# A new order for the opening of a decoder layer: conditioning rows behind the tokens, a fifth weight buffer, and all tokens turned between the first two channel tiles

## The chip, the cores and the metric

The kernel runs on one core of a Trainium2 chip. A core has a matrix engine (TensorE, PE in the profile), a vector engine (VectorE, DVE), a scalar engine (ScalarE, ACT), GpSimd (POOL) and SyncE (SP), which here only issues transfers. Each engine works through its own instructions in order. Sixteen DMA engines move data between the chip's memory (HBM) and the on-chip memory (SBUF). Matmul results go to PSUM.

The metric is the device time of one execution in microseconds (us): the median of several runs.

## What is computed

One layer of a hybrid decoder on 256 tokens with 2048 channels, all in float32, and a final norm. The parts that matter here:

```python
c_act = jax.nn.silu(c)
mod = jnp.dot(c_act, w_ada[l]) + b_ada[l]
shift1, scale1, gate1, shift2, scale2, gate2 = jnp.split(mod, 6, axis=-1)
h = _modulate(_rms_norm(x, norm1_g[l]), shift1, scale1)
proj = jnp.einsum("bsd,de->bse", h, w_in[l])
lru_x, lru_gate, q, k, v, g_a, g_b = jnp.split(proj, split_idx, axis=-1)
...
merged = jax.nn.sigmoid(g_a) * y_a + jax.nn.sigmoid(g_b) * y_b
x = x + gate1[:, None, :] * jnp.einsum("bsd,de->bse", merged, w_out[l])
h2 = _modulate(_rms_norm(x, norm2_g[l]), shift2, scale2)
ff = jnp.square(jax.nn.relu(jnp.einsum("bsd,df->bsf", h2, w_ff1[l])))
x = x + gate2[:, None, :] * jnp.einsum("bsf,fd->bsd", ff, w_ff2[l])
...
return _rms_norm(x, final_g)
```

`_rms_norm` divides each token by the root of its mean square and multiplies by a gain; `_modulate` is `h * (1 + scale) + shift`. Before the first weight of `w_in` can be used, the kernel therefore needs the statistics of all tokens, and for each tile of 128 channels its shift and its scale, each a product of the conditioning vector with 128 rows of `w_ada`.

## The kernel before

**Layout.** Channels lie on the 128 partitions in 16 tiles (`KT = 16`), tokens along the free dimension (256). The tokens come as rows, so they are turned on TensorE: four quarters of 512 channels, each quarter two channel tiles.

**Precision.** A float32 product is made of three faster ones: weight and activation are each split into a rounded part and a rest (`wh`, `wl`; `h[j][:, 0]`, `h[j][:, 1]`), and three of the four products are added. For a weight tile ACT makes the rounded part (L161) and DVE the rest (L163), in halves of 1024 columns; for a channel tile L146 and L147. One kind of unit, the native one (L206), uses the raw weights and needs no split.

**Conditioning.** A row of `w_ada` for one tile is 128 x 2048 values, 1 MB, and is multiplied with the line of the activated conditioning vector (`scr`) and summed on DVE (L287, `ada_unit`). There are 96 such rows; rows 0 and 1 are the shift and scale of channel tile 0, rows 2 and 3 those of tile 1, and so on.

**Buffers.** Conditioning rows and weight tiles share one tag (`raw`), with `RAW_BUFS = 4` buffers of 1 MB. A transfer into a buffer is issued on SP's queue once the buffer's last reader is done: L287 for a conditioning row, L163 for a weight tile. The tokens lie first in the buffers of `wh` and `wl`. Pairs of channel tiles (normalised tokens, their splits, results) share the pool `kp` with 49 buffers.

**The opening**, in program order: the vector table `vc` and the identity `idt` come on ACT's queue, the tokens in four transfers on SP's, and behind them conditioning rows 0 and 1, the first weights, and row 2. The conditioning line is made by four groups of transposes (`line_quarter`, L225, L226), between which DVE and ACT sum the squares of the tokens (L229, L233). `rstd_cols` makes the factors `rs1`. `turn_in(q)` scales a quarter (DVE for the first 128 tokens, L254, ACT for the others, L255), turns it by 8 transposes (L261) and evicts it by two copies (L263). `norm1_tile(j)` makes the factor of tile j on DVE (L301), applies it on ACT (L303) and splits the tile.

**The order.** `pin` (`keep_in_program_order`) keeps the marked instructions of an engine in the order of the program. The rest, the matmuls among it, is put in order by a scheduler when the kernel is built, by priority (program order) and by when its model expects an instruction's inputs; it also hands out the pool's buffers as they come free. The pinned order of the opening is the last part of the code below, L307 to L323.

**Passes and units.** The input projection begins before all channel tiles exist: `PASSES = [(0, 2, 56), (2, 6, 56), (6, 10, 40)]` goes over channel tiles 0 and 1 for 56 output tiles, then 2 to 5, then 6 to 9; a pass evicts or adds its part into `res` (L372, L374, L376). One transfer of 1 MB is a unit: 7 in pass 1, 14 in pass 2, 10 in pass 3. In pass 1 a unit is 8 output tiles by 2 channel tiles by 3 matmuls, 48 in all, with 4 PSUM banks for the output tiles. Between units conditioning rows are reduced (`ADA_FIRST`), those of rows 4 to 11 pinned. Then come the rest of the projection, attention and recurrence, the two branch projections, the output projection, and four groups of feed-forward units; the remaining conditioning rows are spread among them.

Of the kernel before, what the change touches and what calls it, by code (L numbers as in the profile page):

```python
# [58 lines left out]
def hybrid_layer(ctx: ExitStack, tc: tile.TileContext, x, xt, wada, w_p, w_r, w_f, vec, lruw, relb,  # L59
# [22 lines left out]
    def tmp(shape=(P, 2, T), dt=F32):  # L82
        return tp.tile(list(shape), dt, tag="t2", name=nm("t"))
# [59 lines left out]
    def split(src, pin=lambda i: i):  # L143

        hl = pair(F32R)
        pin(se.activation(hl[:, 0], src, AF.Copy))  # L146
        pin(ve.tensor_tensor(out=hl[:, 1], in0=src, in1=hl[:, 0].bitcast(F32), op=ALU.subtract))  # L147
        return hl


    def w_dma(src, n, pin=lambda i: i):
        raw = wp.tile([P, 2048], F32, tag="raw", name=nm("rw"), bufs=RAW_BUFS)
        pin(nc.sync.dma_start(out=raw[:, :n], in_=src))
        return raw, n

    def w_split(raw, n, pin=lambda i: i, o0=0):
        parts = []
        for o in range(o0, o0 + n, WCH):
            c = min(WCH, o0 + n - o)
            wh = wp.tile([P, WCH], F32R, tag="wh", name=nm("wh"), bufs=WH_BUFS)  # L160
            pin(se.activation(wh[:, :c], raw[:, o:o + c], AF.Copy))  # L161
            wl = wp.tile([P, WCH], F32R, tag="wl", name=nm("wl"), bufs=WH_BUFS)
            pin(ve.tensor_tensor(out=wl[:, :c], in0=raw[:, o:o + c], in1=wh[:, :c].bitcast(F32), op=ALU.subtract))  # L163
            parts.append((wh, wl))
# [55 lines left out]
    def line_quarter(q):  # L220
# [4 lines left out]
            te.transpose(pc[:, i * P:(i + 1) * P], sc[:, k:k + 1].broadcast_to((P, P)), idt)  # L225
        pin(se.activation(scr[:, q * 512:(q + 1) * 512], pc, AF.Copy))  # L226

    def square_dve(b, q):
        pin(ve.tensor_tensor_reduce(out=tmp([P, 512]), in0=xtok[b, q], in1=xtok[b, q], scale=1.0, scalar=0.0,  # L229
                                    op0=ALU.mult, op1=ALU.add, accum_out=ssq[:, b, q:q + 1]))  # L230

    def square_act(b, q):
# [16 lines left out]
    rs1 = rstd_cols(ss1, pin)  # L249
    xs = []  # L250

    def turn_in(q):

        pin(ve.tensor_scalar(out=xtok[0, q], in0=xtok[0, q], scalar1=rs1[:, 0:1], scalar2=None, op0=ALU.mult))  # L254
        pin(se.activation(xtok[1, q], xtok[1, q], AF.Copy, scale=rs1[:, 1:2]))  # L255
        for j in (2 * q, 2 * q + 1):
            px = bank([P, 512])
            for i in range(2):
                for b in range(2):
                    e = (2 * (j % 2) + i) * P  # L260
                    te.transpose(px[:, i * T + b * P:i * T + (b + 1) * P], xtok[b, q][:, e:e + P], idt)  # L261
            xs.append(pair())
            pin(se.activation(xs[j].rearrange("p a b -> p (a b)"), px, AF.Copy))  # L263
# [4 lines left out]
    same = lambda i: i  # L268

    def ada_dma(pin=same):  # L270
        raw = wp.tile([P, KT * P], F32, tag="raw", name=nm("ra"), bufs=RAW_BUFS)
        pin(nc.sync.dma_start(out=raw, in_=wada[ada_next[0] + len(ada_raw)]))
        ada_raw.append(raw)

    ada_raw = []

    def ada_unit(pin=same):
# [7 lines left out]
        if 2 * PASSES[0][1] <= n < 2 * PASSES[0][1] + 8:  # L285
            pin = tc.keep_in_program_order
        pin(ve.tensor_tensor_reduce(out=raw, in0=raw, in1=scr, scale=1.0, scalar=vc[:, V_BADA + c:V_BADA + c + 1],  # L287
                                    op0=ALU.mult, op1=ALU.add, accum_out=mod[:, c:c + 1]))
        return n

# [3 lines left out]
    def ada_norm1():  # L294
        n = ada_unit()
        if n % 2 == 1:
            norm1_tile(n // 2)

    def norm1_tile(j, pin=same):
        xj = xs[j // 2][:, j % 2]  # L300
        pin(ve.scalar_tensor_tensor(out=a1[:, j:j + 1], in0=mod[:, KT + j:KT + j + 1], scalar=1.0,  # L301
                                    in1=vc[:, V_G1 + j:V_G1 + j + 1], op0=ALU.add, op1=ALU.mult))
        pin(se.activation(xj, xj, AF.Identity, scale=a1[:, j:j + 1], bias=mod[:, j:j + 1]))  # L303
        h[j] = split(xj, pin)
# [633 lines left out]
```

## Time and profile before

| | us |
|---|---|
| median of 3 runs | 1588.19 |
| lowest, highest | 1587.64, 1589.57 |
| the profiled execution | 1585.86 |
| its span, first to last instruction | 1584.1 |
| mean granted clock of TensorE | 0.992 of full |

How to read the rows in the prediction: a timeline row gives the start, the duration, the engine, the line of the code, the operation, what it writes and reads, how many instructions are merged, and in brackets how long the engine was idle before it and what released it. A row of a view by stretches gives the stretch, its length, and busy time and number of instructions of each engine; then the granted clock of TensorE (1.00 is full), the busy share of the DMA engines, and GB/s. A row "A <- B: x, n, y" of the list of waits says that A waited for B for x us in n times, the longest y.

### The profile page before, as it was taken

What the parts mean: (1) busy time and instruction counts of PE and PEld (TensorE: products, weight loads), DVE (VectorE), ACT (ScalarE), POOL (GpSimd) and SP (SyncE); (2) the same over time, 40 slices, a digit from 0 to 9 for tenths busy, and PEclk for the clock granted to TensorE, in tenths of its full rate; (3) what the DMA queues carried; (4) which work ended last, traced back from release to release, by engine and by line L of the source; (5) the groups of instructions that cost most, each with busy time, mean ns of one, the idle gap of its engine ahead of it and who ended that gap; (6) DMA issues with size and microseconds to landing.
All of it is one profiled execution on the core that took longest, in us unless ns stands there. A gap on an engine that the chain in (4) does not pass through costs nothing.

```text
span 1584.1 us, 24932 instructions
## 1 busy us (share of the span) xinstructions
PE 1543.9 (97%) x9812; PEld 1383.8 (87%) x9812; DVE 1216.9 (77%) x1941; ACT 890.9 (56%) x1510; POOL 0.2 (0%) x4
## 2 busy tenths in 40 slices
PE   4999999999999999999999999999999999999997
PEld 4999998899988888888889988888888888888886
DVE  5898998898989879788898877965665556655664
ACT  5733447687796564445455863356434663356553
POOL 0000000000000000000000000000000000000000
PEclk7999999999999999999999999999999999999999
DMA  8998976557767768777886666875555555555552
GB/s 324 343 341 321 337 277 210 204 181 242 282 247 291 266 240 301 283 292 288 322 313 239 229 247 249 331 256 190 194 192 189 190 186 186 186 186 188 188 188 75
DMA packets 61126, 387.90 MB, mean 245 GB/s; under 512 B 6512, under 2 KB 10960, under 8 KB 18640
## 3 DMA queue, kind: packets, MB, share of 16 engines
q1 hardware_dynamic: 55728, 380.66, 66.1%
q10 hardware_dynamic: 5280, 5.64, 1.2%
q8 instruction: 77, 1.26, 0.3%
q14 instruction: 41, 0.34, 0.1%
HBM read 384.13 MB, written 2.15 MB: 244 GB/s over the span
## 4 chain that ended last, share of the span: by engine, by line
PE 86%; DVE 5%; DMA 4%; issue 3%; ACT 2%; ACTq 0%; DVEq 0%
PE pg L191 41%; PE pg L190 20%; PE pg L179 5%; PE pg L177 5%; PE pg L178 5%; DMA ra<-in_wada_dram 3%; DVE wl L163 2%; PE pg L206 2%; PE pg L193 1%; PE pg L727 1%; PE pg L728 1%; PE pg L726 1%; DVE ra L287 1%; PE pa L532 1%; PE pa L539 1%
## 5 line engine op out<-in xcount | busy, mean ns | idle before, releaser
L191 PE MATMUL pg<-k,wh 128*128 128x512 f32 x3120 | 1076.0, 394 | 0.3 <-DVE k L147 0.3
L163 DVE TENSOR_TENSOR wl<-rw,wh 128x1024 fp32r<-128x1024 f32 (+2 forms) x534 | 628.3, 1179 | 266.1 <-ACT wh L161 259.8
L161 ACT ACTIVATE wh<-rw 128x1024 fp32r<-128x1024 f32 (+2 forms) x534 | 545.0, 1022 | 509.0 <-PE pg L191 353.3
L190 PE MATMUL pg<-k,wl 128*128 128x256 f32 x2925 | 818.9, 280 | 0.6 <-DVE wl L163 0.6
L191 PEld LDWEIGHTS pg<-k,wh 128*128 128x128 f32 x3120 | 572.6, 188 | 118.9 <-PE pg L191 0.6
L190 PEld LDWEIGHTS pg<-k,wl 128*128 128x128 f32 x2925 | 550.3, 188 | 10.4 <-DVE wl L163 0.9
L177 PE MATMUL pg<-k,wh 128*128 128x256 f32 x832 | 237.6, 287 | 7.4 <-ACT k L146 5.7
L179 PE MATMUL pg<-k,wl 128*128 128x256 f32 x832 | 233.6, 284 | 3.6 <-DVE wl L163 3.6
L287 DVE CUSTOM_DVE_ANT_0 ra<-ra,scr,vc 128x2048 f32<-128x2048 f32 x96 | 225.1, 2346 | 14.4 <-DMA ra<-in_wada_dram 14.3
L178 PE MATMUL pg<-k,wh 128*128 128x256 f32 x832 | 234.2, 282 | 0.0
L177 PEld LDWEIGHTS pg<-k,wh 128*128 128x128 f32 x832 | 157.5, 190 | 10.0 <-ACT k L146 6.5
L179 PEld LDWEIGHTS pg<-k,wl 128*128 128x128 f32 x832 | 156.5, 189 | 6.2 <-DVE wl L163 4.9
L178 PEld LDWEIGHTS pg<-k,wh 128*128 128x128 f32 x832 | 157.5, 189 | 0.7 <-issue 0.3
L754 DVE SCALAR_TENSOR_TENSOR k<-pg,mod,k 128x256 f32<-128x256 f32 x128 | 61.9, 484 | 31.7 <-PE pg L191 29.5
L743 ACT ACTIVATE t<-t 128x256 f32<-128x256 f32 x55 | 23.0, 419 | 68.0 <-DVE t L198 67.8
L193 PE MATMUL pg<-k,wl 128*128 128x256 f32 x195 | 54.7, 281 | 2.0 <-DVE wl L163 2.0
L198 DVE TENSOR_TENSOR t<-pg,t 128x256 f32<-128x256 f32 x131 | 54.8, 418 | 0.0
L197 ACT ACTIVATE t<-pg 128x256 f32<-128x256 f32 x131 | 47.8, 365 | 1.7 <-PE pg L191 1.7
L193 PEld LDWEIGHTS pg<-k,wl 128*128 128x128 f32 x195 | 36.6, 188 | 10.8 <-DVE wl L163 2.8
L727 PE MATMUL pg<-z,wh 128*128 128x256 f32 x144 | 41.0, 285 | 0.0
L726 PE MATMUL pg<-z,wh 128*128 128x258 f32 x144 | 40.7, 282 | 0.0
L728 PE MATMUL pg<-z,wl 128*128 128x258 f32 x144 | 40.6, 282 | 0.0
(161 smaller groups left out, 963.1 us busy)
## 6 DMA issues: line engine op xcount, KB each, us to landing
rw<-in_w_f_dram SPq DMA_DIRECT2D x204, 1024.0 KB, 4.8
ra<-in_wada_dram SPq DMA_DIRECT2D x96, 1024.0 KB, 6.2
rw<-in_w_p_dram SPq DMA_DIRECT2D x31, 1024.0 KB, 6.4
rw<-in_w_r_dram SPq DMA_DIRECT2D x20, 768.0 KB, 4.5
rw<-in_w_r_dram SPq DMA_DIRECT2D x16, 640.0 KB, 3.9
bt<-ud ACTq DMA_DIRECT2D x8, 512.0 KB, 4.0
lw<-in_lruw_dram SPq DMA_DIRECT2D x4, 512.0 KB, 5.9
k<-in_x_dram SPq DMA_DIRECT2D x8, 256.0 KB, 6.0
```

Source lines behind the costliest of these rows:

```text
L161: pin(se.activation(wh[:, :c], raw[:, o:o + c], AF.Copy))
L163: pin(ve.tensor_tensor(out=wl[:, :c], in0=raw[:, o:o + c], in1=wh[:, :c].bitcast(F32), op=ALU.subtract))
L177: te.matmul(ps, lhsT=wh[:, w], rhs=hl[:, 0], start=k == 0, stop=False)
L178: te.matmul(ps, lhsT=wh[:, w], rhs=hl[:, 1], start=False, stop=False)
L179: te.matmul(ps, lhsT=wl[:, w], rhs=hl[:, 0], start=False, stop=k == n - 1)
L190: te.matmul(ps[:, 0], lhsT=wl[:, w], rhs=hl[:, 0], start=False, stop=False)
L191: te.matmul(ps, lhsT=wh[:, w], rhs=hl, start=k == 0, stop=k == n - 1)
L193: te.matmul(ps[:, 0], lhsT=wl[:, w], rhs=hl[:, 0], start=False, stop=False)
L287: pin(ve.tensor_tensor_reduce(out=raw, in0=raw, in1=scr, scale=1.0, scalar=vc[:, V_BADA + c:V_BADA + c + 1], op0=ALU.mult, op1=ALU.add, ac ...
L726: te.matmul(ps, lhsT=wh[:, e], rhs=z[k][:, 0:258], start=k == 0, stop=False)
L727: te.matmul(ps[:, 0:256], lhsT=wh[:, e], rhs=z[k][:, 258:514], start=False, stop=False)
L754: ve.scalar_tensor_tensor(out=x1[f], in0=ps[:, i], scalar=mod[:, 5 * KT + f:5 * KT + f + 1], in1=x1[f], op0=ALU.mult, op1=ALU.add)
```

## The change

It has four parts.

1. `RAW_BUFS` goes from 4 to 5; `kp` from 49 to 48 buffers.
2. The vector table is sent on SP's queue ahead of the tokens instead of on ACT's, where the identity is then alone.
3. The first raw buffer is taken early, and the first square of the tokens (L229) writes its unused result into it. So the transfer of conditioning row 0 into that buffer, and what stands behind it on SP's queue, is issued after this square. Four conditioning rows (0 to 3) instead of three are asked for in the opening.
4. The pinned order of the opening is new. `turn_in`, `w_split` and `norm1_tile` are taken apart (`scale_in`, `w_round` and `w_rest`, `norm1_rest`), and the pieces are put so that quarters 1, 2 and 3 are turned between channel tiles 0 and 1, with the DVE scales of quarters 2 and 3 ahead of the reduce of row 2. Rows 0 to 11 are pinned as before.

```diff
-RAW_BUFS, WH_BUFS, WCH = 4, 3, 1024
+RAW_BUFS, WH_BUFS, WCH = 5, 3, 1024
...
-    kp = ctx.enter_context(tc.tile_pool(name="kp", bufs=49))
+    kp = ctx.enter_context(tc.tile_pool(name="kp", bufs=48))
...
-    pin(se.dma_start(out=vc, in_=vec))
+    pin(nc.sync.dma_start(out=vc, in_=vec))
...
+    ada_raw = [wp.tile([P, KT * P], F32, tag="raw", name=nm("ra"), bufs=RAW_BUFS)]
+
     def square_dve(b, q):
-        pin(ve.tensor_tensor_reduce(out=tmp([P, 512]), in0=xtok[b, q], ...
+        pin(ve.tensor_tensor_reduce(out=ada_raw[0][:, 0:512] if b + q == 0 else tmp([P, 512]), in0=xtok[b, q], ...
...
+    def turn_in(q, step=None):
+
+        if not step:
+            scale_in(0, q)
+            scale_in(1, q)
+        if step is False:
+            return
         for j in (2 * q, 2 * q + 1):
...
     ada_dma(pin)
     ada_dma(pin)
     first_raw = w_dma(w_p[0], 2048, pin)
     ada_dma(pin)
+    ada_dma(pin)
     turn_in(0)
-    turn_in(1)
-    ada_unit(pin)
-    n1 = ada_unit(pin)
-    first_w = w_split(first_raw[0], WCH, pin)
-    norm1_tile(n1 // 2, pin)
-    ada_dma(pin)
-    ada_unit(pin)
+    turn_in(1, False)
+    ada_unit()
+    ada_unit()
+    whs = w_round(first_raw[0], 0, WCH, pin)
+    norm1_tile(0, pin)
+    turn_in(1, True)
+    scale_in(0, 2)
+    scale_in(0, 3)
+    first_w = [w_rest(first_raw[0], 0, WCH, whs, pin)]
+    norm1_rest(0, pin)
+    ada_unit()
     first_w += w_split(first_raw[0], WCH, pin, WCH)
-    n1 = ada_unit(pin)
-    turn_in(2)
-    norm1_tile(n1 // 2, pin)
-    turn_in(3)
+    for q in (2, 3):
+        scale_in(1, q)
+        turn_in(q, True)
+    ada_unit()
+    norm1_tile(1, pin)
+    norm1_rest(1, pin)
```

More of the change, by code (lines that the diff above doesn't have):

```diff
@@ L154, in w_dma, with w_round, w_rest @@
         return raw, n
+    def w_round(raw, o, c, pin=lambda i: i):
+        wh = wp.tile([P, WCH], F32R, tag="wh", name=nm("wh"), bufs=WH_BUFS)
+        pin(se.activation(wh[:, :c], raw[:, o:o + c], AF.Copy))
+        return wh
+    def w_rest(raw, o, c, wh, pin=lambda i: i):
+        wl = wp.tile([P, WCH], F32R, tag="wl", name=nm("wl"), bufs=WH_BUFS)
+        pin(ve.tensor_tensor(out=wl[:, :c], in0=raw[:, o:o + c], in1=wh[:, :c].bitcast(F32), op=ALU.subtract))
+        return wh, wl
     def w_split(raw, n, pin=lambda i: i, o0=0):
@@ L159, in w_split @@
             c = min(WCH, o0 + n - o)
[L160 to L164, printed above, removed]
+            parts.append(w_rest(raw, o, c, w_round(raw, o, c, pin), pin))
         return parts
@@ L226, in line_quarter @@
         pin(se.activation(scr[:, q * 512:(q + 1) * 512], pc, AF.Copy))
+    ada_raw = [wp.tile([P, KT * P], F32, tag="raw", name=nm("ra"), bufs=RAW_BUFS)]
     def square_dve(b, q):
-        pin(ve.tensor_tensor_reduce(out=tmp([P, 512]), in0=xtok[b, q], in1=xtok[b, q], scale=1.0, scalar=0.0,
+        pin(ve.tensor_tensor_reduce(out=ada_raw[0][:, 0:512] if b + q == 0 else tmp([P, 512]), in0=xtok[b, q], in1=xtok[b, q], scale=1.0, scalar=0.0,
                                     op0=ALU.mult, op1=ALU.add, accum_out=ssq[:, b, q:q + 1]))
@@ L250, in hybrid_layer, with scale_in @@
     xs = []
-    def turn_in(q):
-        pin(ve.tensor_scalar(out=xtok[0, q], in0=xtok[0, q], scalar1=rs1[:, 0:1], scalar2=None, op0=ALU.mult))
-        pin(se.activation(xtok[1, q], xtok[1, q], AF.Copy, scale=rs1[:, 1:2]))
+    def scale_in(b, q):
+        if b == 0:
+            pin(ve.tensor_scalar(out=xtok[0, q], in0=xtok[0, q], scalar1=rs1[:, 0:1], scalar2=None, op0=ALU.mult))
+        else:
+            pin(se.activation(xtok[1, q], xtok[1, q], AF.Copy, scale=rs1[:, 1:2]))
+    def turn_in(q, step=None):
[4 more added lines that the diff above has]
+            return
         for j in (2 * q, 2 * q + 1):
@@ L270, in ada_dma, with ada_unit @@
     def ada_dma(pin=same):
[L271 to L277, printed above, removed]
+        n = ada_next[0] + len(ada_raw)
+        if n == 1 and not ada_in[0]:
+            ada_in[0] = True
+            n, raw = 0, ada_raw[0]
+        else:
+            raw = wp.tile([P, KT * P], F32, tag="raw", name=nm("ra"), bufs=RAW_BUFS)
+            ada_raw.append(raw)
+        pin(nc.sync.dma_start(out=raw, in_=wada[n]))
+    ada_in = [False]
+    def ada_unit():
         if not ada_raw:
@@ L283, in ada_unit @@
         c = ADA_ORDER[n]
-        if 2 * PASSES[0][1] <= n < 2 * PASSES[0][1] + 8:
-            pin = tc.keep_in_program_order
-        pin(ve.tensor_tensor_reduce(out=raw, in0=raw, in1=scr, scale=1.0, scalar=vc[:, V_BADA + c:V_BADA + c + 1],
+        (pin if n < 2 * PASSES[0][1] + 8 else same)(ve.tensor_tensor_reduce(out=raw, in0=raw, in1=scr, scale=1.0, scalar=vc[:, V_BADA + c:V_BADA + c + 1],
                                     op0=ALU.mult, op1=ALU.add, accum_out=mod[:, c:c + 1]))
@@ L297, in ada_norm1 @@
             norm1_tile(n // 2)
+            norm1_rest(n // 2)
     def norm1_tile(j, pin=same):
@@ L303, in norm1_tile, with norm1_rest @@
         pin(se.activation(xj, xj, AF.Identity, scale=a1[:, j:j + 1], bias=mod[:, j:j + 1]))
-        h[j] = split(xj, pin)
+        h[j] = pair(F32R)
+        pin(se.activation(h[j][:, 0], xj, AF.Copy))
+    def norm1_rest(j, pin=same):
+        xj = xs[j // 2][:, j % 2]
+        pin(ve.tensor_tensor(out=h[j][:, 1], in0=xj, in1=h[j][:, 0].bitcast(F32), op=ALU.subtract))
     ada_dma(pin)
```

## The prediction

> **What bounds the kernel now.** The page comes first: who is busy, and where TensorE is not.
>
> ```profile
> span 1584.1 us, 24932 instructions
> PE 1543.9 (97%) x9812; PEld 1383.8 (87%) x9812; DVE 1216.9 (77%) x1941; ACT 890.9 (56%) x1510; POOL 0.2 (0%) x4
> ```
>
> TensorE is idle for 1584.1 - 1543.9 = 40.2 us. The view by stretches says where.
>
> ```profile
> core 0: us, PE busy (x) PEld busy (x) DVE busy (x) ACT busy (x) POOL busy (x), PEclk, DMA share, GB/s
> 0.00:39.20 39.20, 18.67 (x97) 16.58 (x98) 22.09 (x40) 21.36 (x41) 0.20 (x4) 0.74 0.85 327
> 72.00:210.00 138.00, 136.51 (x1039) 132.03 (x1038) 126.97 (x190) 52.27 (x63) 0.00 (x0) 1.00 0.91 336
> ```
>
> Half of the idle time, 39.20 - 18.67 = 20.5 us, is in the opening; the passes (72 to 210) have 1.5. In the opening TensorE also runs on a granted clock of 0.74. What the opening waits for stands in the timelines of the three engines, DVE first, then ACT, then PE.
>
> ```profile
> 12.99 0.88 DVE L254 TENSOR_SCALAR wh<-wh,st 128x512 f32<-128x512 f32 x2
> ...
> 21.81 0.43 DVE L147 TENSOR_TENSOR k<-k,k 128x256 fp32r<-128x256 f32 x1 [1.18 <-ACT k L146]
> 22.15 2.35 DVE L287 CUSTOM_DVE_ANT_0 ra<-ra,scr,vc 128x2048 f32<-128x2048 f32 x1
> 24.42 1.22 DVE L163 TENSOR_TENSOR wl<-rw,wh 128x1024 fp32r<-128x1024 f32 x1
> 25.56 2.35 DVE L287 CUSTOM_DVE_ANT_0 ra<-ra,scr,vc 128x2048 f32<-128x2048 f32 x1
> 27.83 0.48 DVE L254 TENSOR_SCALAR wh<-wh,st 128x512 f32<-128x512 f32 x1
> 28.23 0.15 DVE L301 SCALAR_TENSOR_TENSOR a<-mod,vc 128x1 f32<-128x1 f32 x1
> ```
>
> ```profile
> 17.12 1.24 ACT L263 ACTIVATE k<-pa 128x512 f32<-128x512 f32 x2 [0.99 <-PE pa L261]
> 18.25 1.05 ACT L161 ACTIVATE wh<-rw 128x1024 fp32r<-128x1024 f32 x1
> 20.73 0.60 ACT L303 ACTIVATE k<-k,mod,a 128x256 f32<-128x256 f32 x1 [1.42 <-DVE a L301]
> 22.63 0.71 ACT L255 ACTIVATE wl<-wl,st 128x512 f32<-128x512 f32 x1
> 29.54 0.60 ACT L263 ACTIVATE k<-pa 128x512 f32<-128x512 f32 x1 [6.20 <-PE pa L261]
> 30.89 0.59 ACT L303 ACTIVATE k<-k,mod,a 128x256 f32<-128x256 f32 x1
> ```
>
> ```profile
> 23.74 0.41 PE L179 MATMUL pg<-k,wl 128*128 128x256 f32 x1
> 23.95 0.41 PE L177 MATMUL pg<-k,wh 128*128 128x256 f32 x1
> 28.41 0.45 PE L261 MATMUL pa<-idt,wh 128*128 128x128 f32 x1 [3.62 <-issue]
> 31.98 1.22 PE L177 MATMUL pg<-k,wh 128*128 128x256 f32 x4 [1.62 <-ACT k L146]
> 39.17 0.28 PE L177 MATMUL pg<-k,wh 128*128 128x256 f32 x1
> 39.29 0.28 PE L178 MATMUL pg<-k,wh 128*128 128x256 f32 x1
> ```
>
> The reader is to see a knot. The token scale of quarter 2 (27.83) stands on DVE behind the conditioning reduces of 22.15 and 25.56. TensorE's next instructions are that quarter's transposes, so it waits until 28.41; ACT's next is their eviction, so it waits 6.20 us. Channel tile 1 has its factor at 28.23 but is made on ACT only at 30.89, behind those evictions. TensorE gets tile 1 at 31.98, and starts unit 1 of the weights at 39.17. From there it is busy without a gap through pass 1, so what the opening saves is read as an earlier unit 1.
>
> **The change, part by part.** *Evictions and scales out of the knot.* The new order puts the scales of quarters 2 and 3 (two L254 instructions) ahead of the third reduce and all transposes ahead of tile 1. I work the new times out on ACT, which now has the longest queue. Its first weight rounding (L161) needs the weight tile:
>
> ```profile
> L153 SPq DMA_DIRECT2D rw<-in_w_p_dram x1: 328/328/328, 5.4 to 5.4; - x1
> ...
> DMA to landing us min/median/max: 11.5/11.5/11.5
> ...
> L272 SPq DMA_DIRECT2D ra<-in_wada_dram x1: 431/431/431, 5.8 to 5.8; - x1
> ...
> DMA to landing us min/median/max: 13.6/13.6/13.6
> ```
>
> It lands at 5.4 + 11.5 = 16.9; today the rounding starts at 18.25 only because two evictions (17.12) precede it. Now it runs 17.0 to 18.0. DVE has made the factor of tile 0 by then or shortly after: from 12.99 two scales, two reduces of 2.27 each and L301 give 18.5 at the latest, 17.1 if the token statistics come 1.4 us earlier (below). I take tile 0's L303 at 18.05. It takes 0.6 and the rounding of the tile 0.4, so TensorE has tile 0 at about 19.1. ACT goes on: two evictions 1.1 (from 19.0 to 20.1), the second weight rounding 0.95, the scale of quarter 2 0.7 (to 21.75), transposes and evictions of that quarter, the scale of quarter 3 0.7, its transposes and evictions. Such a quarter takes 30.89 - 28.41 = 2.48 from the first transpose to the next ACT instruction where both halves of the tokens start together; the one evicted from 17.12 took some 2.1. I take 2.3. So tile 1's L303 starts at 21.75 + 2.3 + 0.7 + 2.3 = 27.05 (ends 26.6 and 27.4). DVE is ready: from its latest 18.5, two scales 0.8, the subtract 1.14, tile 0's low half 0.34, reduce, subtract, reduce 2.27 + 1.14 + 2.27 give 26.5. TensorE started 31.98 - 30.89 = 1.09 after L303, so now at 28.15: 3.8 us earlier.
>
> *What TensorE then has left.* Before, 12 matmuls of tile 1 (four outputs by three), the 8 transposes of quarter 3 and 24 matmuls lay between 31.98 and 39.17. Now the transposes are done and 36 matmuls remain. They are 0.21 apart on the slow clock (23.74 to 23.95) and 0.12 on the full one (39.17 to 39.29). The clock:
>
> ```profile
> 24.00:28.00 4.00, 0.79 (x4) 0.49 (x3) 4.00 (x6) 0.00 (x0) 0.00 (x0) 0.50 0.63 219
> 32.00:36.00 4.00, 3.85 (x20) 3.65 (x20) 3.05 (x4) 1.81 (x4) 0.00 (x0) 0.64 0.49 207
> ```
>
> A mean of 0.64 over four microseconds means 0.5 for 2.9 us and 1.0 for the rest: it rose 2.9 us after the work of 31.98 began. With the same delay now, 14 matmuls take 2.9 and 22 take 2.6, together 5.5, so unit 1 starts at 28.15 + 5.5 = 33.65. Ends: all slow 7.6 (35.75), all at full clock 4.3 (32.45). Against 39.17 the term is **-5.5 us**, between -3.4 and -6.7.
>
> The Trainium skill, "TensorE: Matmul & The Clock Gate", Part 1, says that the gate knows only half and full rate and opens after a busy window of about 3.4 us; this speaks against an order that feeds TensorE in shorter bursts. The rows agree on 0.5 and 1.0. By its 3.4 us, unit 1 would start some 0.2 us later than I reckon.
>
> *Conditioning rows behind the tokens.* The first square now writes into the first conditioning buffer, so that buffer's transfer waits on SP for DVE, and behind it on that queue stand three more conditioning rows and the first weights; DVE's reduces and ACT's rounding wait for those.
>
> ```profile
> 5.75 0.68 DVE L229 CUSTOM_DVE_ANT_0 t<-wh 128x512 f32<-128x512 f32 x1
> ...
> 11.56 0.16 DVE L248 TENSOR_REDUCE ss<-ssq 128x2 f32<-128x8 f32 x1 [1.41 <-ACT t L233]
> ```
>
> The first square ends at 6.4 today, so these issue from 6.4 on, at some 0.4 apart, the weights third at about 7.3 instead of 5.4. Cost between nothing and that delay, 1.9. I take nothing: the two transfers above were issued 0.4 us apart and landed 2.5 apart (16.9 and 19.4), so the rate paces them, not the issue, as long as the tokens ahead fill the engines until then.
>
> *Vector table on SP, identity alone on ACT's queue.* The identity's landing gates the first transposes:
>
> ```profile
> PE pa L225 <- DMA idt<-in_ident_dram: 7.0, 1, 7.0
> ```
>
> Sooner, it brings the statistics forward by at most the 1.41 that DVE waited for ACT's squares at 11.56; later, by the 0.4 that one more issue on SP puts ahead of the tokens. In the sum it moves tile 0 by 0.5 at most, since the weights land at 16.9 anyway.
>
> *Fifth weight buffer.* What is late next? The weights of unit 1 had to wait for the third reduce's buffer, free at 24.5. Now they take the second's, free at about 18, and at 2.5 us a transfer land by about 27, in time for 33.65; their split on DVE follows the fifth reduce, 28.6 + 2.3 + 1.1 = 32.0. From there on every engine has the same work as before, 5.5 us sooner. The stalls that are left:
>
> ```profile
> 81.87 0.38 PE L179 MATMUL pg<-k,wl 128*128 128x256 f32 x1 [0.74 <-DVE wl L163]
> 87.93 0.39 PE L177 MATMUL pg<-k,wh 128*128 128x256 f32 x1 [0.50 <-ACT wh L161]
> 362.60 0.39 PE L179 MATMUL pg<-k,wl 128*128 128x256 f32 x1 [1.68 <-DVE wl L163]
> 388.55 0.39 PE L179 MATMUL pg<-k,wl 128*128 128x256 f32 x1 [0.97 <-DVE wl L163]
> 444.91 0.39 PE L193 MATMUL pg<-k,wl 128*128 128x256 f32 x1 [1.97 <-DVE wl L163]
> ```
>
> and, from the list of waits, ACT's between 75 and 210:
>
> ```profile
> ACT wh L161 <- DMA rw<-in_w_p_dram: 34.0, 10, 6.2
> ```
>
> The two near 85 come from weights that landed late (ACT waited 34.0 us for them in the passes). An earlier issue can take 0.74 + 0.50 = 1.2 away, or nothing; nothing speaks for either end, so half, **-0.6**. One channel buffer fewer (48): I count 48 live at the most at the branch gates and at the first feed-forward units, so nothing; if one unit waits there it is a tail of about 2 us like the 1.97 above.
>
> Sum: -5.5 - 0.6 = -6.1. The profiled execution took 1585.86 for its span of 1584.1; so a span near 1578.0, and from the median of 1588.2 a time of **1582.1**.
>
> **The rivals.** *Given back in the passes.* The stretch from 72 to 210 runs with DVE at 92% and DMA at 0.91; a head start of 5.5 us helps only if both come along. If the transfers keep their old times, TensorE waits in pass 2 and all but the 0.6 is lost: 1587.6; with half of it lost, 1584.9. For it: the 34.0 us of ACT waiting. Against it: DMA ran at 0.63 and 0.49 in the two stretches quoted with the clock, 3.5 us of idle transfer time that the earlier issues fill.
>
> *Slower: reduces ahead of splits.* In the three stalls of 362.60, 388.55 and 444.91 a weight split stood on DVE behind a reduce of 2.3 us; they cost 1.54 each on average. Reduces from the 13th on are not pinned, 84 of them, and the scheduler orders them by when their data come; a fifth buffer brings them earlier and can put more of them ahead of splits. Four more eat the gain, and from seven on the kernel is slower: 1582.1 + 7 x 1.54 = 1592.9. Against it: of those 84, three cost something today.
>
> *Better than forecast.* Full clock for the 36 matmuls (-6.7) and both late landings gone (-1.2): 1580.3, and 1578.8 if one of the split stalls, 1.54, goes too.
>
> *The held-back rows cost their issue delay.* Then tile 1 comes 1.9 later: 1584.0.
>
> **How the numbers follow.** Forecast 0.55, given back 0.17, better 0.12, slower 0.10, held-back rows 0.06. 0.2% of 1588.2 is 3.2 us, about what a measurement of this kernel can tell from no change; so faster means below 1585.0. Faster: 0.52 + 0.12 + 0.05 + 0.03 = 0.72; within: 0.18; slower: 0.10. The range reaches from 1578.5 to 1587.0: up to most of the given-back case, leaving out its end and the slower one.
>
> **What would show it.** Right: unit 1 starts near 33.7 (32.4 to 35.8), the long wait of 3.62 is gone, ACT's chain from the first weight rounding at 17 is unbroken but for transposes, pass 2 starts 5 to 6 us sooner than before. Wrong: first weights landing well after 17; unit 1 early but a TensorE wait for a split in pass 2; new waits behind reduces after 210; or pairs of channel buffers waiting for a matmul.

## The result, and the profile after

The changed kernel takes 1595.22 us (median of 5 runs, 1594.10 to 1595.90), the kernel before 1588.19 in the runs beside it (1586.18 to 1590.47). The ratio is 1.0040, interval 1.0024 to 1.0055: **slower**, by some 7 us, where 6 us faster was forecast. The profiled execution of the changed kernel took 1595.22, of which 1593.4 are its span. The row of busy times of its page and its row of conditioning reduces, and then that row of the kernel before:

```profile
PE 1554.2 (98%) x9812; PEld 1386.8 (87%) x9812; DVE 1218.3 (76%) x1941; ACT 895.9 (56%) x1514; POOL 0.2 (0%) x4
...
L309 DVE CUSTOM_DVE_ANT_0 ra<-ra,scr,vc 128x2048 f32<-128x2048 f32 x96 | 225.0, 2345 | 1.3 <-DMA ra<-in_wada_dram 1.2
```

```profile
L287 DVE CUSTOM_DVE_ANT_0 ra<-ra,scr,vc 128x2048 f32<-128x2048 f32 x96 | 225.1, 2346 | 14.4 <-DMA ra<-in_wada_dram 14.3
```

The fifth buffer does what it says: DVE stood idle 14.4 us ahead of its conditioning reduces before, 1.3 us now. TensorE is idle 1593.4 - 1554.2 = 39.2 us, not more than the 40.2 of before; the longer span shows as longer busy time, in matmuls that follow each other more slowly. The opening ends earlier, but pass 1 gives it back. The view by stretches, first of the changed kernel (to unit 1, and from there to pass 2), then of the kernel before (pass 1 alone):

```profile
0.00:36.70 36.70, 20.17 (x97) 17.89 (x98) 21.59 (x40) 21.59 (x42) 0.20 (x4) 0.67 0.94 365
36.70:75.00 38.30, 36.06 (x291) 34.59 (x290) 29.47 (x31) 29.32 (x65) 0.00 (x0) 1.00 0.80 298
```

```profile
39.20:73.20 34.00, 34.00 (x291) 33.99 (x290) 29.68 (x31) 28.44 (x66) 0.00 (x0) 1.00 0.92 337
```

Pass 1 lasts 38.3 us instead of 34.0, with the same 291 matmuls. TensorE's timeline shows where channel tile 1 arrives, and the new holes, two in pass 1 and three later. The two in pass 1 cost 2.4 us with the slower start behind each; the rest of the 4.3 lies in pauses of 0.1 to 0.2 us between single matmuls.

```profile
30.78 1.22 PE L183 MATMUL pg<-k,wh 128*128 128x256 f32 x4 [1.62 <-ACT k L328]
...
43.81 0.38 PE L183 MATMUL pg<-k,wh 128*128 128x256 f32 x1 [1.07 <-ACT wh L158]
...
57.04 0.38 PE L183 MATMUL pg<-k,wh 128*128 128x256 f32 x1 [1.07 <-ACT wh L158]
...
484.01 0.49 PE L197 MATMUL pg<-k,wh 128*128 128x512 f32 x1 [1.03 <-ACT wh L158]
...
485.85 0.39 PE L199 MATMUL pg<-k,wl 128*128 128x256 f32 x1 [1.34 <-DVE wl L163]
...
924.95 0.89 PE L196 MATMUL pg<-k,wl 128*128 128x256 f32 x3 [1.42 <-ACT k L146]
```

A wide unit is one whose matmuls take both parts of the activation at once (L196 to L199). How far each point is behind the profiled execution of before (starts of the same matmuls; units counted from the first wide unit, the one near 420 us, as number 0):

```
                          unit 1   pass 2   wide 4   wide 10  wide 76  wide 79  last
before, starts at          39.17    73.16   444.91   482.20   905.66   922.65  1574.69
changed kernel             -2.50    +1.80    -0.51    +3.65    +3.75    +7.69    +9.93
```

So: 2.5 us gained in the opening, 4.3 lost in pass 1, 2.1 gained at 445 where a stall went, 4.2 lost by wide unit 10, 3.9 lost at 925, and 2.1 lost slowly after 950. The execution of before is a quick one (1585.86 against a median of 1588.2), so the last column says more than 7.

### The profile page after: what moved, and what is told of

The parts are those of the page before. It is cut to its first block, busy times and chain, and to the rows that moved or that the text cites. A ratio compares the mean times of both kernels' runs of the same rounds, so it can differ in the third digit from the quotient of the medians.

```text
span 1593.4 us, 24931 instructions
## 1 busy us (share of the span) xinstructions
PE 1554.2 (98%) x9812; PEld 1386.8 (87%) x9812; DVE 1218.3 (76%) x1941; ACT 895.9 (56%) x1514; POOL 0.2 (0%) x4
## 4 chain that ended last, share of the span: by engine, by line
PE 88%; DVE 5%; ACT 4%; DMA 1%; issue 1%; SPq 0%; ACTq 0%; DVEq 0%
PE pg L197 44%; PE pg L196 21%; PE pg L185 5%; PE pg L183 5%; PE pg L184 5%; PE pg L212 2%; DVE wl L163 2%; PE pg L199 1%; ACT wh L158 1%; DVE ra L309 1%; DMA rw<-in_w_p_dram 1%; PE pg L762 1%; PE pg L761 1%; PE pg L763 1%; PE pa L567 1%
## 5 line engine op out<-in xcount | busy, mean ns | idle before, releaser
L163 DVE TENSOR_TENSOR wl<-rw,wh 128x1024 fp32r<-128x1024 f32 (+2 forms) x534 | 628.1, 1178 | 280.9 <-ACT wh L158 275.1
L158 ACT ACTIVATE wh<-rw 128x1024 fp32r<-128x1024 f32 (+2 forms) x534 | 544.1, 1021 | 509.4 <-PE pg L197 369.9
L196 PE MATMUL pg<-k,wl 128*128 128x256 f32 x2925 | 817.8, 280 | 1.6 <-ACT k L146 1.4
L196 PEld LDWEIGHTS pg<-k,wl 128*128 128x128 f32 x2925 | 551.0, 188 | 11.6 <-ACT k L146 2.6
L199 PE MATMUL pg<-k,wl 128*128 128x256 f32 x195 | 55.0, 282 | 1.4 <-DVE wl L163 1.3
L199 PEld LDWEIGHTS pg<-k,wl 128*128 128x128 f32 x195 | 36.6, 188 | 11.4 <-DVE wl L163 3.1
```

The lines of the kernel that those rows point to most:

```text
L196: te.matmul(ps[:, 0], lhsT=wl[:, w], rhs=hl[:, 0], start=False, stop=False)
L199: te.matmul(ps[:, 0], lhsT=wl[:, w], rhs=hl[:, 0], start=False, stop=False)
```

## The experiments

Times are medians of 5 rounds unless "one run" is said. Each ratio is to the kernel before in the same series, whose medians lay between 1588.44 and 1588.85; intervals are of 95%.

**The opening without the fifth buffer.**

```diff
-RAW_BUFS, WH_BUFS, WCH = 5, 3, 1024
+RAW_BUFS, WH_BUFS, WCH = 4, 3, 1024
...
-    kp = ctx.enter_context(tc.tile_pool(name="kp", bufs=48))
+    kp = ctx.enter_context(tc.tile_pool(name="kp", bufs=49))
```

> The changed kernel with 4 weight buffers and 49 channel buffers again; the new opening alone. Theory A (the losses have two separate places: the opening, +1.8 us at the start of pass 2, and the fifth buffer's new order of DVE and ACT behind the passes, about +5): pass 2 starts about 1.8 later than before (near 75), nothing is lost at 484 and 925, the time is near 1590. Rival B (everything comes from the opening, which shifts all that follows): the stalls behind the passes stay, the time stays near 1595.

Measured: 1591.04, ratio 1.0013 (1.0001 to 1.0025). No stall at 484 or 925, but unit 1 only 2.8 us sooner and pass 2 1.7 later, as in the changed kernel. So the opening as changed is itself no gain, and what is lost at 482 and 925 isn't its doing.

**The fifth buffer without the opening** (the kernel before).

```diff
-RAW_BUFS, WH_BUFS, WCH = 4, 3, 1024
+RAW_BUFS, WH_BUFS, WCH = 5, 3, 1024
...
-    kp = ctx.enter_context(tc.tile_pool(name="kp", bufs=49))
+    kp = ctx.enter_context(tc.tile_pool(name="kp", bufs=48))
```

> The kernel before with 5 weight buffers and 48 channel buffers, its opening untouched. Theory A: pass 2 starts within 1 us of before (73.2), the stalls near 484 and 925 are there, the time is near 1593. Rival B: the same as before, 1588, or a little faster for the stalls near 85.

Measured: 1597.94, ratio 1.0057 (1.0042 to 1.0072), more than expected. The two stalls near 484 are there, and the one at 926 with a low clock. TensorE's timeline, and the stretch from 922 to 934 in this kernel and then in the kernel before:

```profile
483.60 0.49 PE L191 MATMUL pg<-k,wh 128*128 128x512 f32 x1 [1.03 <-ACT wh L161]
485.50 0.39 PE L193 MATMUL pg<-k,wl 128*128 128x256 f32 x1 [1.41 <-DVE wl L163]
```

```profile
922.00:934.00 12.00, 10.38 (x49) 8.44 (x48) 9.59 (x14) 9.25 (x20) 0.00 (x0) 0.86 0.59 197
```

```profile
922.00:934.00 12.00, 12.00 (x71) 10.49 (x70) 9.22 (x12) 7.32 (x13) 0.00 (x0) 1.00 0.70 263
```

In the same 12 us TensorE runs 49 matmuls instead of 71: a stall of 1.4 us and a granted clock of 0.86 on the mean. The fifth buffer alone costs as much as the whole change or more. The stalls at 484 and near 925 stand in all five profiles with five buffers and the scheduler's order, and in none of those with four. How those at 484 come about is seen in ACT's and DVE's timelines of the changed kernel:

```profile
479.27 1.28 ACT L672 ACT_TABLE_LOAD   x1
...
480.99 1.28 ACT L631 ACT_TABLE_LOAD   x1
482.28 0.73 ACT L631 ACTIVATE t<-t 128x256 f32<-128x256 f32 x2
482.91 1.99 ACT L158 ACTIVATE wh<-rw 128x1024 fp32r<-128x1024 f32 x2
```

```profile
478.85 2.35 DVE L309 CUSTOM_DVE_ANT_0 ra<-ra,scr,vc 128x2048 f32<-128x2048 f32 x1
...
484.59 2.34 DVE L163 TENSOR_TENSOR wl<-rw,wh 128x1024 fp32r<-128x1024 f32 x2
```

and in those of the kernel before, the same rounding and the same reduce (the 147th and the 49th of the program in both):

```profile
476.59 1.06 ACT L161 ACTIVATE wh<-rw 128x1024 fp32r<-128x1024 f32 x1 [0.67 <-PE pg L191]
```

```profile
483.12 2.35 DVE L287 CUSTOM_DVE_ANT_0 ra<-ra,scr,vc 128x2048 f32<-128x2048 f32 x1
```

The reduce of 2.35 us comes two weight splits earlier than before, ahead of the recurrence's work; on ACT the recurrence and the gate alternate between two function tables, and the weight rounding (L158) comes behind two table loads of 1.28 us, at 482.91 instead of 476.59. From 400 to 500 us these two lines load six times each instead of four; one of them, before and after:

```profile
L596 ACT ACT_TABLE_LOAD x4 | 5.1, 1283 | 0.1
```

```profile
L631 ACT ACT_TABLE_LOAD x6 | 7.7, 1283 | 0.1
```

The Trainium skill, "ScalarE: Activation LUTs", What ACT_TABLE_LOAD costs, gives some 1283 ns for a load; the trace agrees to the nanosecond.

**The conditioning rows not held back.**

```diff
-    ... out=ada_raw[0][:, 0:512] if b + q == 0 else tmp([P, 512]), ...
+    ... out=tmp([P, 512]), ...
```

> The changed kernel, only that the first square writes into a temporary again, so the conditioning rows and first weights are issued at once behind the tokens. Theory C (holding them back leaves the DMA engines with too little queued, and so the tokens land late, 12.2 instead of 9.4): last tokens at 9.4 to 9.8, first weights at about 17, unit 1 starts 2 to 3 us sooner than 36.7, the time is 1592 to 1593. Rival D (the vector table ahead of the tokens on SP's queue delays them): tokens still land at 12, time 1595.

Measured: 1596.93, ratio 1.0050 (1.0035 to 1.0065); the second 128 tokens land at 10.9 and 12.2, the first weights at 19.6, as in the changed kernel, though the rows are issued from 3.1 us on instead of 6.2. Holding the rows back shows neither gain nor loss here, and it isn't what makes the tokens late.

**The vector table back on ACT's queue.**

```diff
-    pin(nc.sync.dma_start(out=vc, in_=vec))
+    pin(se.dma_start(out=vc, in_=vec))
```

> The changed kernel, only that the vector table goes on ACT's queue ahead of the identity again. Rival D: last tokens land at about 9.4 to 10, the time falls by 2 to 3 us to about 1592.5. Theory C: the last tokens still land after 11.5, the time stays within 1 us of 1595.2.

Measured: 1594.72, ratio 1.0034 (1.0023 to 1.0046): only 0.5 us less, where 2 to 3 were expected. The transfers of the second 128 tokens (issue, then time to landing), in the changed kernel, in this one, and in one more, told next:

```profile
L99 SPq DMA_DIRECT2D wl<-in_xt_dram x2: 424/428/432, 1.6 to 2.6; - x2
...
DMA to landing us min/median/max: 8.0/8.8/9.6
```

```profile
L99 SPq DMA_DIRECT2D wl<-in_xt_dram x2: 421/564/707, 1.2 to 2.1; - x2
...
DMA to landing us min/median/max: 5.5/6.5/7.4
```

```profile
L98 SPq DMA_DIRECT2D wl<-in_xt_dram x2: 422/427/432, 1.2 to 2.1; - x2
...
DMA to landing us min/median/max: 4.9/6.0/7.0
```

With the table ahead of them on SP's queue the last tokens land at 2.6 + 9.6 = 12.2, with it on ACT's at 2.1 + 7.4 = 9.5. Unit 1 starts at 32.89 instead of 36.67, and ACT's first rounding at 17.33 instead of 19.64:

```profile
17.33 1.06 ACT L158 ACTIVATE wh<-rw 128x1024 fp32r<-128x1024 f32 x1 [0.27 <-DMA rw<-in_w_p_dram]
...
27.39 0.60 ACT L326 ACTIVATE k<-k,mod,a 128x256 f32<-128x256 f32 x1
```

```profile
19.64 1.06 ACT L158 ACTIVATE wh<-rw 128x1024 fp32r<-128x1024 f32 x1 [1.39 <-DMA rw<-in_w_p_dram]
```

**The vector table on SP's queue, but behind the tokens.**

```diff
-    pin(nc.sync.dma_start(out=vc, in_=vec))
...
                 xtok[b, 2 * i + q] = xh[:, q * 512:(q + 1) * 512]
+    pin(nc.sync.dma_start(out=vc, in_=vec))
```

> The changed kernel, with the vector table behind the four token transfers on SyncE's queue instead of ahead of them. Theory D1 (what stands ahead of the tokens on their queue delays them): the tokens land as in the kernel before, the last two at 8.2 and 9.5, and the table only near 9 to 10, so that the modulation line is late and the first reduce starts 1 to 2 us later than with the table on ScalarE's queue. Theory D2 (it is the rate: with nearly all transfers on one queue less is moved, wherever the table stands): the tokens land at 10 to 12 as in the changed kernel.

Measured (one run): 1597.30. The third fence above is this kernel's: the tokens land by 2.1 + 7.0 = 9.1. So it is the place ahead of the tokens that counts, not the queue. The table itself lands at 9.6, which delays the conditioning line and the square that releases the held-back transfers: the first weights land at 20.4, and unit 1 starts at 35.39.

**Four buffers and the table on ACT's queue.**

```diff
-RAW_BUFS, WH_BUFS, WCH = 5, 3, 1024
+RAW_BUFS, WH_BUFS, WCH = 4, 3, 1024
...
-    pin(nc.sync.dma_start(out=vc, in_=vec))
+    pin(se.dma_start(out=vc, in_=vec))
```

> The changed opening with four weight buffers (and 49 pair tiles), and the vector table back on ScalarE's queue ahead of the identity. Theory A+D+E (fifth buffer, table ahead of the tokens, ScalarE's order in pass 1 each cost their own): unit 1 starts near 33 (6 ahead of before), pass 2 near 71.2 (2 ahead, the other 4.3 lost in pass 1 by ScalarE's order), no stall at 484 nor at 925, and the end 1.5 to 3 us ahead of before: 1585 to 1587. Rival (only the fifth buffer costs, the table's place is worth nothing in the end): as the opening alone was, about 1591. Rival (the earlier start is given back whatever the order, because later stalls have fixed places in the transfers): 1588 to 1589.

Measured: 1589.56, ratio 1.0004 (0.9994 to 1.0014): no more loss, and none of the expected gain. Unit 1 started at 35.90 here, not at 32.89, with the same order up to there. Channel tile 1 reached TensorE at 28.98 instead of 28.49; the rest of the difference is the clock. The stretch from 28 to 34 us, first of the table-on-ACT kernel above, then of this one:

```profile
28.00:34.00 6.00, 5.51 (x44) 5.34 (x45) 4.11 (x5) 4.67 (x11) 0.00 (x0) 1.00 1.02 423
```

```profile
28.00:34.00 6.00, 5.02 (x23) 5.02 (x24) 2.69 (x3) 3.21 (x8) 0.00 (x0) 0.50 0.98 362
```

The clock behind tile 1 is worth 2.5 us of unit 1 and isn't the same in like programs. (The view reads 1.00 also where a profile has no record of the clock: the record of the table-on-ACT profile begins at 23.59, and its matmuls lie 0.21 us apart until then, as on half clock, and 0.12 later.) Pass 1 still took 38.1 us, with its two stalls.

**Pass 1 with ACT's order fixed.** Cause to be tested: ACT's order in pass 1. In the changed kernel the scheduler puts the rounding for the next unit behind the preparation of a channel tile (L326, L328), in ACT's timeline:

```profile
41.64 0.59 ACT L326 ACTIVATE k<-k,mod,a 128x256 f32<-128x256 f32 x1
...
42.40 0.41 ACT L328 ACTIVATE k<-k 128x256 fp32r<-128x256 f32 x1
42.70 1.05 ACT L158 ACTIVATE wh<-rw 128x1024 fp32r<-128x1024 f32 x1
```

TensorE wants that half of the weights at 42.7 and gets it at 43.81. In the kernel before the same rounding came ahead of the tile preparation:

```profile
39.82 1.13 ACT L161 ACTIVATE wh<-rw 128x1024 fp32r<-128x1024 f32 x1
...
44.23 0.61 ACT L303 ACTIVATE k<-k,mod,a 128x256 f32<-128x256 f32 x1 [0.23 <-DVE a L301]
```

The edit, on the kernel just told (four buffers, table on ACT's queue), rounds it early:

```diff
...
+                wts = first_w if n_pass == 1 else ahead or w_split(*raw)
+                nxt, ahead = w_dma(w_p[n_pass], 2048)[0] if k0 == 0 and u + per < n else None, []
                 for i in range(nf):
                     add_part(gemm(wts, i * kw, h[k0:k1]), u + i)
+                    if nxt is not None and i in (1, 4):
+                        o = WCH * len(ahead)
+                        ahead.append(w_rest(nxt, o, WCH, w_round(nxt, o, WCH, pin)))
```

> As the run before it, and in pass 1 ScalarE rounds the next unit's weights after the second and the fifth eviction of this one (kept in program order), ahead of the tile preparation of the unit's end. Theory E (pass 1 lost 4.3 us by ScalarE's order alone): the units of pass 1 last 5.65 us each again without the two stalls of 1.03 to 1.07 us, pass 2 starts at 67 to 68, and the time is 3 to 5 us under the run before it: 1581 to 1584, under both kernels. Rival (pass 1 is slower because the weights or the conditioning rows land later, or because the clock is lower): the order changes nothing, pass 2 near 71.

Measured: 1588.76, ratio 1.0002 (0.9992 to 1.0012). Pass 1 took 39.6 us, more than before the edit: the expectation failed. The rounding no longer waits, but now the tile preparation does, at the place where the pin keeps it, and the evictions stand behind it. ACT and then TensorE:

```profile
43.70 0.60 ACT L326 ACTIVATE k<-k,mod,a 128x256 f32<-128x256 f32 x1 [2.59 <-DVE a L324]
```

```profile
45.07 0.39 PE L183 MATMUL pg<-k,wh 128*128 128x256 f32 x1 [1.56 <-ACT k L407]
```

ACT waited 2.59 us for DVE's reduce. TensorE ran on into its four PSUM banks and then waited 1.56 us for an eviction.

**The tile preparation one unit later** (on the same kernel).

```diff
+                    if i == 4:
+                        while owed:
+                            j = owed.pop(0)
+                            norm1_tile(j, pin)
+                            norm1_rest(j)
...
+                m = ada_unit()
+                if m % 2 == 1 and k0 == 0 and u + per < n:
+                    owed.append(m // 2)
...
```

> The opening with four weight buffers and the table on ScalarE's queue; in pass 1 the weight rounding after the second and the fifth eviction, and the tile preparation that follows a reduce moved into the next unit, behind its fifth eviction. Theory E (any ScalarE instruction that waits in its order holds the evictions behind it, and four PSUM buffers cover some 2 us of that): neither weight rounding nor tile scale waits, the units last 5.65 us each with no stall over 0.7 us, pass 2 starts 34.0 us after unit 1 (39.6 in the run of the fixed order before, 38.1 with the scheduler's), so at 67 to 70 with the clock that the opening gets; time 3 to 5 us under the 1588.8 of that run: 1584 to 1586. Rival (pass 1 is bound by VectorE's reduces and splits or by landing weights): pass 2 still 38 us behind unit 1, time 1588 to 1590.

Measured: 1589.07, ratio 1.0008 (0.9993 to 1.0023). The same two rows:

```profile
47.19 0.60 ACT L326 ACTIVATE k<-k,mod,a 128x256 f32<-128x256 f32 x1 [1.09 <-DVE a L324]
```

```profile
48.56 0.38 PE L183 MATMUL pg<-k,wh 128*128 128x256 f32 x1 [0.57 <-ACT k L407]
```

Pass 1 took 35.7 us (34.0 were expected), and pass 2 started at 70.80, 2.4 us ahead of the first profile of before. So of the 4.1 us that pass 1 lost with four buffers (38.1 against 34.0), 2.4 come back by the order of weight split and tile preparation alone; what is left is mostly the tile preparation, which still waits about 1.1 us twice. The median doesn't show it: this profile has its last matmul 1.7 us behind that of before, having lost 1.5 between pass 2 and 420 us and 2.3 after 950, and the twelve runs fall in two groups (1584.9 to 1589.6, and 1593.0 to 1595.7).

**Five buffers, with the reduces one unit later** (the kernel before, five buffers).

```diff
-        while ada_credit > 0 and ada_next[0] < 6 * KT:
-            ada_unit()
+        for _ in range(owed):
+            ada_unit()
+        owed = 0
+        while ada_credit > 0 and ada_next[0] + owed < 6 * KT:
+            owed += 1
             ada_credit -= 1
```

> The kernel before with five weight buffers and 48 pair tiles, and each wide unit's conditioning reduces emitted one unit later. Theory A1 (the fifth buffer costs because the scheduler puts the reduces, and with them ScalarE's table loads, ahead of weight splits and tile preparations): the order near 444 to 497 is the old one again, the stalls at 484 and 485 go, wide unit 12 starts at most 1 us later than with four buffers (with five it was 5.0 later); the last reduce ahead of the sixteenth normalised tile stays, and with it the 2.5 to 4 us at 925: 1591 to 1593 against 1597.9 of the fifth buffer alone. Rival A2 (the fifth buffer costs by its transfers, earlier loads that collide, or by the 48 pair tiles): the stalls stay, 1597 to 1599.

Measured: 1592.29, ratio 1.0019 (1.0010 to 1.0027), 5.6 us under the fifth buffer alone. The list of TensorE's waits from 470 to 500 us has one entry left, and the timeline near 925 still its stall:

```profile
PE pg L193 <- DVE wl L163: 0.8, 1, 0.8
```

```profile
923.32 0.63 PE L190 MATMUL pg<-k,wl 128*128 128x256 f32 x3 [1.63 <-ACT k L146]
```

So at 484 it was the early reduces; what they do directly and what through ACT's table loads isn't separated (the line quoted with four loads before and six in the changed kernel has five here).

**Five buffers, without reduces near the last normalised tiles** (the same kernel, without the edit just shown).

```diff
-        if n_ff1 - QUIET_OUT <= n < n_ff1 or n_ff1 + 16 - ...
+        if n_ff1 - QUIET_OUT <= n < n_ff1 or n_ff1 + 6 <= n < n_ff1 + 13 or n_ff1 + 16 - ...
```

> The kernel before with five weight buffers and 48 pair tiles, and no conditioning reduces emitted in the seventh to the thirteenth unit of the first feed-forward block. Theory A1: the stall at 922 to 927 and the low clock behind it go (the reduce of 2.35 us stands no longer ahead of the sixteenth normalised tile), the units there start as many us late as unit 76 does, no more; the stalls at 484 stay: 4 us under the fifth buffer alone, 1593 to 1595. Rival A2 (not the reduce): stays at 1597 to 1599.

Measured: 1595.29, ratio 1.0045 (1.0029 to 1.0060). The reduces are gone and a stall stays:

```profile
927.63 0.39 PE L190 MATMUL pg<-k,wl 128*128 128x256 f32 x1 [1.32 <-DVE wl L163]
```

The low clock behind it went, and with it 1.4 of 3.9 us. The rest isn't the reduce. What is left is seen in DVE's timeline, first here, then in the kernel before, where the sixteenth normalised tile is begun:

```profile
923.30 0.42 DVE L687 TENSOR_TENSOR t<-k,rs 128x256 f32<-128x256 f32 x1
```

```profile
910.79 0.42 DVE L687 TENSOR_TENSOR t<-k,rs 128x256 f32<-128x256 f32 x1
```

It is 12.5 us late, though the unit there is only 5.6 us late (unit 76). So the tile lags 6.9 us behind its unit; in the six other profiles with five buffers told of so far it lags 7.9 to 8.2 us, in those with four buffers not at all (0.02 us at most). On DVE 301 weight splits (L163) stand ahead of it with five buffers and 299 with four, and in the changed kernel one more reduce. Without that reduce the lag is 1.2 us shorter.

**Three normalised tiles per unit instead of two** (with the reduces one unit later).

```diff
-            for k in (2 * f, 2 * f + 1):
+            for k in range(3 * f, 3 * f + 3):
```

> The kernel before with five weight buffers and 48 pair tiles, each wide unit's conditioning reduces emitted one unit later, and three normalised tiles made per feed-forward unit instead of two. Theory A3 (near 925 not the reduce itself but the lag of the normalised tiles behind weight splits stalls TensorE: with five buffers the sixteenth is started at 921 to 924 instead of 910.8): the sixteenth is started by 912, the stall of 1.3 to 1.6 us at 923 to 928 goes, units 76 to 84 keep their distance (with the reduces later alone it grew by 3.8), 1588 to 1590 against 1592.3. Rival A1 (the reduce): the reduce still stands near the last tiles, the stall stays, 1592.

Measured: 1599.47, ratio 1.0061 (1.0046 to 1.0077). It failed: the added work delays the unit's own results, and TensorE stalls earlier.

```profile
905.55 0.55 PE L726 MATMUL pg<-z,wh 128*128 128x258 f32 x1 [3.38 <-DVE t L732]
917.62 0.47 PE L191 MATMUL pg<-k,wh 128*128 128x512 f32 x1 [3.38 <-DVE t L732]
```

**The whole change with these mends:** five buffers, and the edits shown for the table, pass 1 (both), the reduces and the tiles. Their first lines:

```diff
+    pin(se.dma_start(out=vc, in_=vec))
...
+                    if nxt is not None and i in (1, 4):
...
+                    if i == 4:
...
+        for _ in range(owed):
...
+            for k in range(3 * f, 3 * f + 3):
```

> The whole change with its three losses mended: five weight buffers, the table on ScalarE's queue, pass 1 with fixed rounding and the tile preparation one unit later, reduces one unit later, three normalised tiles per unit. If the causes found are all of them, the gain of the opening (pass 2 near 69 to 71 against 73 to 74.5 of before) reaches the end and the stalls at 445, 484 and 925 are gone: 1583 to 1586, under both kernels. Rival (what is gained early is lost in the long stretch by a slower pace of the same matmuls, 1 to 2.7 us, or by lower clocks behind other stalls): 1587 to 1590.

Measured: 1600.00, ratio 1.0066 (1.0052 to 1.0081): the same two stalls of 3.38 us. Up to 830 us it was 0.6 us ahead of the quick profile of before, where the changed kernel was 3.3 behind.

**The same, but two tiles per unit, and the tiles needed one unit later.**

```diff
-ZN_FROM = 9
+ZN_FROM = 10
```

> The whole change mended as before, but with two normalised tiles per unit as in the changed kernel, and ten instead of nine feed-forward units that multiply the unnormalised tiles, so that the normalised ones are needed one unit later. Theory A3 (the sixteenth normalised tile comes too late for unit 9): with one unit of 5.65 us more the stall at 923 to 928 goes, the units from 72 to 84 keep their distance to within 1.5 us, and what the mended opening and the fifth buffer gain until unit 72 (0.6 us ahead of the faster execution of before, 6 ahead of the slower) stays up to the pace of the long stretch: 1584 to 1588. Rival (the tiles are late by more than a unit, or the longer life of the unnormalised tiles stalls the 48 pair tiles): 1590 or more.

Measured: **1587.97**, ratio 0.9992 (0.9981 to 1.0002). All of TensorE's waits from 470 to 960 us:

```profile
PE pg L199 <- DVE wl L163: 0.7, 1, 0.7
PE pg L197 <- DVE k L147: 0.3, 1, 0.3
```

The stall at 925 is gone, which moving the reduces alone had left (1.63 us), so there the lag of the normalised tiles was the cause. The mended change is 7 us under the changed kernel and as fast as the kernel before, not measurably faster. `ZN_FROM = 10` was not tried in the kernel before, so how much of the 7 us it would give there isn't known.

**The kernel before, once more,** and **with one more transpose.**

```diff
+    pin(te.transpose(bank([P, 512])[:, :P], idt, idt))
     line_quarter(0)
```

> The kernel before, unchanged, for a second profiled execution beside the first. If the 1.5 to 2 us by which every other profile fell behind the first one after 950 us belong to that one execution, this profile falls behind it there as well, and its own opening may differ by the granted clock between 14 and 34 us; if they belong to the changes, it agrees with the first within 0.5 us at every mark.

> The kernel before with one more 128x128 transpose on TensorE in the opening, whose result is not read; every other instruction is in the old order. From 950 to 1565 both executions of before took the same to 0.03 us, the changed programs 1.0 to 2.7 us more, with no stall. Theory P1 (where TensorE's instructions lie in its stream sets the pace by hundredths of a microsecond a unit): this stretch is 0.5 us or more off that of before. Theory P2 (the pace comes from the order or the timing of the other engines' work): it takes what it took before, to 0.1 us.

Measured (one run each): 1592.25 and 1591.52. In the second profile of before unit 1 starts at 40.43, 1.3 us later than in the first, and the profile falls 4.7 us behind the first between pass 2 and 420 us: the stall that the first has at 388.55 with 0.97 us is 3.04 us long, and the clock falls behind it.

```profile
392.91 0.58 PE L179 MATMUL pg<-k,wl 128*128 128x256 f32 x1 [3.04 <-DVE wl L163]
```

```profile
388.00:400.00 12.00, 8.96 (x63) 8.75 (x63) 9.91 (x17) 8.46 (x18) 0.00 (x0) 0.86 0.64 218
```

From wide unit 84 to the last one, 110 units, the two profiles of before take 615.01 and 615.04 us, the one with the transpose 615.00. The changed kernel takes 617.14, its opening with four buffers 615.93, the last kernel of pass 1 617.33, all without a stall and at a granted clock of 1.00. One more TensorE instruction ahead doesn't make it, and a different order needn't either: of the opening with four buffers the last 500 instructions of each computing engine stand in the same order as in the kernel before, and it takes 0.9 us more. Whether they use the same buffers isn't in the traces. The cause stays open.

## Why the prediction was wrong

**The opening term, -5.5.** In the changed kernel it was -2.5. Channel tile 1 reached TensorE at 30.78, 2.6 us later than the 28.15 forecast, and the 36 matmuls behind it took 5.9 us instead of 5.5. Where the tokens come in time the chain is as forecast: with the table on ACT's queue the first rounding starts at 17.33 (17.0), tile 1's L326 at 27.39 (27.05), and tile 1 reaches TensorE at 28.49 (28.15). Unit 1 is then a matter of the clock: 32.89 with the 36 matmuls at full clock (forecast for that case 32.45), and 35.90, in the kernel with four buffers, with most of them at half (35.75). So the order in the opening was worked out rightly, and its input, the landing of the tokens and weights, was wrong.

**The step that failed first: vector table on SP.** "In the sum it moves tile 0 by 0.5 at most, since the weights land at 16.9 anyway." I counted one more issue of 0.4 us. The queue showed more: the last tokens 2.7 us later (12.2 against 9.5 with the table on ACT's queue), and the first weights, behind them on the same queue, at 19.6 instead of 17.3. "The weights land at 16.9 anyway" treated as fixed what stands behind the delayed transfers. Why 176 KB cost 2.7 us isn't shown; from 4 to 8 us the DMA engines moved 239 GB/s in the changed kernel (0.86 busy) against 384 before. TensorE's transposes for the conditioning line fall into the same stretch (3.31 us busy against 0.99), since the identity lands at 3.5 instead of 6.9; which of the two slows the transfers isn't separated.

```profile
4.00:8.00 4.00, 3.31 (x16) 3.07 (x16) 1.31 (x4) 1.61 (x3) 0.00 (x0) 1.00 0.86 239
```

```profile
4.00:8.00 4.00, 0.99 (x5) 1.03 (x6) 1.40 (x5) 1.70 (x3) 0.00 (x0) 1.00 1.00 384
```

**The step that failed most in the passes: "From there on every engine has the same work as before, 5.5 us sooner."** The work was the same, its order was not: pass 1 lost 4.3 us, and the two kernels that moved only the weight split and the tile preparation within it made it 39.6 and 35.7 us long.

**The fifth buffer, -0.6: wrong in sign.** Alone, with one channel buffer fewer, it costs 9.1 us (1597.94 against 1588.83). I took only the two late landings near 85 from it. The rival "reduces ahead of splits" had the object right (with a fifth buffer the scheduler orders DVE's work otherwise) and got a tenth of the chance, because I counted stalls of 1.54 us and asked for seven. It took two places: early reduces and table loads near 484, 5.6 us in the time when moved, and normalised tiles that come too late for the unit at 925, with a lower clock behind the stall. The rival "given back in the passes" named transfers; it was the order of the weight split and the tile preparation on ACT.

**Conditioning rows behind the tokens, nothing:** held, 1596.93 without against 1595.22 with, and the first weights land at 19.6 either way. **48 channel buffers, nothing:** not tried alone, so their share in the cost of the fifth buffer isn't separated; the mended kernel has 48 and is as fast as the kernel before.

**The clock.** I let it rise 2.9 us after tile 1. In the changed kernel it was half from 10.3 to 34.2, so it rose 3.4 us after tile 1, and this has 0.4 of the 3.0 us that the opening term is short; the late tokens have the rest. In the kernel before it was half from 14.4 to 34.9. The row of 0.74 that I quoted for the opening counts 1.00 up to 10.98, where that profile's record of the clock begins, though its transposes there lie 0.21 us apart; nothing in the sum rests on it.

The range ended at 1587.0 and did not hold 1595.2: each term stood by the quoted rows of the old order, and none by what the scheduler would make of the new one.

## What to carry to other kernels

When an order is made by a scheduler, a buffer more or a new opening is a new order for the whole kernel: compare the engines' sequences of both programs before costing a step at "the same work, sooner". A transfer put ahead of others on a queue can delay everything behind it, here the weights too, and is costed by what lands last. On an engine that runs its instructions in order, an instruction pinned early moves the wait to whatever stands behind it, so place both the one that feeds TensorE and the one that waits.

## What was not expected of the hardware

The granted clock halves behind short stalls, and not each time. The stall of 1.97 us at 444.91 in the first profile of before left it at 1.00; in the second, one of 1.95 us at the same place took it to 0.50 for about 3 us, and so did the 1.42 us at 925 in the changed kernel. At 925 it adds some 1.4 us: the kernel with the fifth buffer alone, where the clock falls behind a stall of 1.4 us, loses 3.9 us there, and the one without reduces, where it doesn't fall behind one of 1.3, loses 2.5. It isn't shown to make the spread of some 8 us between runs of one kernel: runs of the kernel before took 1587.47 us at a mean clock of 0.990 and 1590.78 at 0.996. The Trainium skill, "TensorE: Matmul & The Clock Gate", Part 1, lets the clock fall after an idle window of about 3.4 us; these stalls are shorter, and the measurement decides. Second, the same matmuls without a stall and at full clock took 615.0 to 617.3 us for 110 units, the same to 0.04 us in three profiles of one order and another value in other programs.
